# Mixture-of-experts stage: overflow branch behind the eighth pair, unread products, a gather with two writes per bank turn, and a reordered router

## The chip, the cores and the metric

The kernel runs on one core of a Trainium2 chip. A core has five engines with queues of their own: TensorE for matrix products (PE, its weight loads shown apart as PEld), VectorE (DVE), ScalarE (ACT), GpSimd (POOL) and SyncE (SP), which here issues nearly all DMAs. The metric is the device time of one execution in microseconds (us). The kernel before takes 2117.66 us, the median of three runs between 2117.41 and 2118.54.

## The reference, cut to what matters

The program computes two blocks over 256 rows of 1024 columns. The first is a hybrid layer (three attention-like branches, merged by gates) followed by a hierarchical mixture of experts; the second holds two feed-forward parts, a gated unit and a stick-breaking attention. The change touches the mixture of experts alone. A router picks for each row one of four groups and in it the two best of eight experts; all products are dense in the reference, with gates that are zero for the experts that were not picked.

```python
x = x + gt1 * (merged @ w_out)
h2 = rmsnorm(x, norm2_g) * (1.0 + sc2) + sh2
group_logits = h2 @ rg_w + rg_b
g_sel = argmax(group_logits)
exp_logits = (h2 @ re_w + re_b).reshape(-1, 4, 8)
in_group = exp_logits of group g_sel
top_v, top_i = lax.top_k(in_group, 2)
gates = softmax(top_v) * softmax(group_logits)[g_sel], at the picked experts
hg = silu(h2 @ w_gate[e]) * (h2 @ w_up[e])          # 1024 -> 512, 32 experts
y = sum over e of (hg * gates[:, e]) @ w_down[e]    # 512 -> 1024
x = x + gt2 * y
```

The weights of the experts are 32 x 3 matrices of 1024 x 512 (or 512 x 1024) numbers in f32, 201 MB of the 500 MB that the kernel reads.

## The kernel before

**Weights.** The expert weights come as 192 loads of 1 MB (tile 128 x 2048, half of a matrix), each issued by load_slot (L1200) on SP. There are 17 slots (names we, wx, ws, whl, wp by the memory they share); 17 loads go out ahead of the stage, the next one for a slot goes out when the products that read it are done. SP takes its queue in order, so a load that waits for its slot holds those behind it.

**Router.** route() runs once the residual rows x are final. TensorE transposes the two row tiles (turn, L1297), the results are copied out of PSUM to xT (evac: L1305 on ACT, L1303 on DVE; xT shares the buffer named whd), eight products per row tile give the 36 logits (L1313), and DVE scales them by the row's norm (rs, made on POOL in L1316) in L1317. Then a row of small DVE operations finds the experts (sel, L1363), TensorE counts each row's place in its expert's list (L1366 to L1370), and DVE makes the rank. The normed rows are kept as two parts of reduced precision, hh (tile hi, on ACT, L1331 and L1339) and hl (tile lo, on DVE, L1332 and L1364).

**Gather.** Each expert has a list of at most C rows. For four experts at a time, places() (L1158) builds a one-hot matrix from the rank, and gather() multiplies it with the rows: for each of eight column blocks k four products (L1172: hi and lo of two row tiles) into half of a PSUM bank, read by one ACT operation (L1174) into xg. Two blocks k share a bank. Four k make a half gather. The first half of the first gather stands before the first expert product; its second half stands in pair 0 after the first two loads are used; later halves stand one in each pair, a group of four experts ahead.

**Pairs.** Two experts form a pair, each on half of the array's columns. A pair has six calls of both() (L1211), each of which reads two loads in 16 products of 512 columns and then issues two loads: four for gate and up, then two for down. Between them stand the activation, the transposes (L1235, L1242), the half gather (ahead) and the previous pair's spread (L1264, eight products that put the results back to their rows). A list of the PE instructions (self.pe) is chained, so that the scheduler keeps their order.

**Overflow.** After pair p = 0 the kernel flushes that pair's spread, starts a new PE list, and calls overflow(): every engine loads the longest list's length (topi, L1407) and, if it is over C, goes through a slow loop for the rest (L1413). With these inputs it is not: the branch is only jumped over. By the built program SP holds at the end of the branch until every DMA that it issued has landed, which the rows in the next sections show.

**After the stage** residual() adds the result to x, and the first feed-forward part begins with transposes (L419).

Of the kernel before, what the change touches and what calls it, by code (L numbers as in the profile page):

```python
# [8 lines left out]
F32 = mybir.dt.float32  # L9
# [3 lines left out]
AF = mybir.ActivationFunctionType  # L13
OP = mybir.AluOpType
# [6 lines left out]
KT = D // 128  # L21
# [11 lines left out]
NB8 = 9  # L33
WS, WHL, WH2 = 3, 3, 3
NE_B8, NE_MIX, NSLOT = 7, 4, 17
ADA_EVERY, ADA_FROM = 3, 6
FRONT = 4
PADS = 320, 128, 128, 224
# [143 lines left out]
class Program:  # L182
# [280 lines left out]
    def run(self):  # L463
        tc, nc, d = self.tc, self.nc, self.d
        with ExitStack() as es:
            self.main = es.enter_context(tc.tile_pool(name="main", bufs=1))
            self.small = es.enter_context(tc.tile_pool(name="small", bufs=1))
            self.pad(self.small, PADS[0], "pad0")
            self.stg = es.enter_context(tc.tile_pool(name="stg", bufs=3))
            self.psum = es.enter_context(tc.tile_pool(name="psum", bufs=4, space=PSUM))  # L470
            self.dram = es.enter_context(tc.tile_pool(name="scr", bufs=1, space=DRAM))
            main = self.main
            self.cm = main.tile([128, KT], F32, name="cm")
            nc.sync.dma_start(self.cm, d["c"])
            self.x = main.tile([128, 2, 1024], F32, name="x")
            for t in range(2):
                nc.sync.dma_start(self.x[:, t], d["x"][t * 128:t * 128 + 128])
            k0 = main.tile([128, 256], F32, name="k0")
            nc.sync.dma_start(k0, d["k0"])
            self.ident, self.anti = k0[:, :128], k0[:, 128:]  # L480
            self.ones = main.tile([128, 128], F32, name="ones")
            nc.vector.memset(self.ones, 1.0)
            self.mhalf = main.tile([128, 32], F32, name="mhalf")
            nc.vector.memset(self.mhalf, -0.5)
            self.cc = main.tile([128, d["cols"].shape[1]], F32, name="cc")
            nc.sync.dma_start(self.cc, d["cols"])
            self.hi, self.lo = [main.tile([128, KT, S], F32R, name=n) for n in ("hi", "lo")]
            self.modscr = self.dram.tile([6, 1024], F32, name="modscr")
            self.rowp = es.enter_context(tc.tile_pool(name="rowp", bufs=1))
            self.km = self.rowp.tile([128, 320], F32, name="km")  # L490
            eights = ExitStack()
            self.exs = eights.enter_context(tc.tile_pool(name="exs", bufs=1))
            self.slots = [self.exs.tile([128, 2048], F32, name="wp")]
            self.units = [(2 * p + j, u) for p in range(NE // 2) for u in range(6) for j in range(2)]
            self.nload = self.nuse = 0
            self.pad(self.exs, PADS[1], "pad1")
            self.b8p = eights.enter_context(tc.tile_pool(name="b8", bufs=1))
            with tc.tile_pool(name="mix", bufs=1) as self.mix:
                self.hybrid()
            fg = self.row(self.rowp, d["rows"][0:1], name="fg", tag="row", bufs=2)  # L500
            self.experts()
            eights.close()
            self.whx = es.enter_context(tc.tile_pool(name="whx", bufs=1))
            self.pad(self.whx, PADS[2], "pad2")
            self.ffn(0, fg)
            self.dbg("f0", self.x)
            with tc.tile_pool(name="sgu", bufs=1) as self.sgup:
                self.sgu()
            self.dbg("m0", self.x)
            self.ffn(1)  # L510
            self.kvp = es.enter_context(tc.tile_pool(name="kv", bufs=1))
            with tc.tile_pool(name="kvt", bufs=1) as kvt:
                self.ffn(2, between=self.kv(kvt))
            self.dbg("f1", self.x)
            with tc.tile_pool(name="sb", bufs=1) as self.sbp:
                self.stick()
            self.dbg("m1", self.x)
            g = self.row(self.rowp, d["rows"][1:2], name="fing", tag="row", bufs=2)
            self.ffn(3)
            self.last_norm(g)  # L520
# [615 lines left out]
    def experts(self):  # L1136
# [5 lines left out]
        with tc.tile_pool(name="exw", bufs=1) as self.exw:  # L1142
# [20 lines left out]
            def gather(q, ks):  # L1163

                oh, xg = ohs[q], xgs[q % 2]
                parts = [(hz, t) for t in range(2) for hz in (self.hl, self.hh)]
                for k in ks:
                    if k % 2 == 0:
                        both = self.mms().rearrange("p (k a c) -> p k a c", k=2, a=4)
                    ps = both[:, k % 2]  # L1170
                    for i, (hz, t) in enumerate(parts):
                        self.chain(self.pe, nc.tensor.matmul(ps, hz[:, t, k * 128:k * 128 + 128], oh[:, t], start=(i == 0), stop=(i == 3)))  # L1172
                    gain, shift = self.a2c[:, k:k + 1], self.sh2c[:, k:k + 1]
                    nc.scalar.activation(xg[:, k], ps, AF.Identity, bias=shift, scale=gain)  # L1174

            places(0)
            gate, rgs = gates()
# [2 lines left out]
            for p in range(NE // 2):  # L1180
                q, ks = p // 2 + 1, range(4 * (p % 2), 4 * (p % 2) + 4)

                def ahead():
                    if 4 * q < NE:
                        if p % 2 == 0:
                            places(q)
                        gather(q, ks)

                pend = self.pair(p, xgs[p // 2 % 2], ohs[p // 2], gate, yp, pend, ahead, gather)
                if p == 0:  # L1190
                    self.spread(*pend)
                    pend, self.pe = None, []
                    self.overflow(topi, rgs, iota)
            self.spread(*pend)
            self.residual(yp, self.gt2)

    def load_slot(self):

# [68 lines left out]
    def route(self, km):  # L1267
# [27 lines left out]
        def turn(t, q):  # L1295
            for k in range(4 * q, 4 * q + 4):
                ins = nc.tensor.transpose(pss[t][q][:, (k % 4) * 128:(k % 4) * 128 + 128], self.x[:, t, k * 128:k * 128 + 128], self.ident)  # L1297
            return ins

        def evac(t, q):  # L1300
            c = xT[:, t, 4 * q:4 * q + 4].rearrange("p a b -> p (a b)")
            if q and t:
                self.chain(edge[0], V.tensor_copy(c, pss[t][q]))  # L1303
            else:
                self.chain(edge[1], nc.scalar.copy(c, pss[t][q]))  # L1305

        def square(t, h):
            self.chain(edge[1], nc.scalar.activation(junk, self.x[:, t, h * 512:h * 512 + 512], AF.Square, accum_out=ss[:, t, h:h + 1]))

        def logits(t):  # L1310
            pl = pss[t][0][:, :36]
            for k in range(KT):
                nc.tensor.matmul(pl, xT[:, t, k], self.rwa[:, k], start=(k == 0), stop=(k == KT - 1))  # L1313
            V.tensor_scalar(ss[:, t, 0:1], ss[:, t, 0:1], 1.0 / D, EPS, op0=OP.mult, op1=OP.add)
            V.scalar_tensor_tensor(ss[:, t, 1:2], ss[:, t, 1:2], 1.0 / D, ss[:, t, 0:1], op0=OP.mult, op1=OP.add)
            ins = nc.gpsimd.tensor_tensor(out=rs[:, t:t + 1], in0=ss[:, t, 1:2], in1=self.mhalf[:, :1], op=OP.pow)  # L1316
            V.scalar_tensor_tensor(lg[:, t], pl, rs[:, t:t + 1], self.base, op0=OP.mult, op1=OP.add)  # L1317
            return ins
# [8 lines left out]
        turn(1, 0)  # L1327
        square(1, 0)
        self.res(1, 1)
        logits(0)  # L1330
        self.chain(edge[1], nc.scalar.activation(hh[:, 0], self.x[:, 0], AF.Copy, scale=rs[:, 0:1]))  # L1331
        self.chain(edge[0], V.scalar_tensor_tensor(hl[:, 0], self.x[:, 0], rs[:, 0:1], hh[:, 0].bitcast(F32), op0=OP.mult, op1=OP.subtract))  # L1332
        evac(1, 0)
        turn(1, 1)
        evac(1, 1)
        square(1, 1)
        logits(1)
        self.chain(edge[1], nc.scalar.activation(junk[:, :1], self.ones[:, :1], AF.Exp))
        self.chain(edge[1], nc.scalar.activation(hh[:, 1], self.x[:, 1], AF.Copy, scale=rs[:, 1:2]))  # L1339
        self.res = self.rest = self.edge = None  # L1340
# [22 lines left out]
        found = V.tensor_mul(sel.rearrange("p a (g e) -> p a g e", g=4), og4, ssel[:, :, None, :].to_broadcast([128, 2, 4, 8]))  # L1363
        self.no_sync(V.scalar_tensor_tensor(hl[:, 1], self.x[:, 1], rs[:, 1:2], hh[:, 1].bitcast(F32), op0=OP.mult, op1=OP.subtract), found)  # L1364
        pk = self.mms()[:, :2 * NE].rearrange("p (a b) -> p a b", a=2)
        nc.tensor.matmul(pk, earlier, sel, start=True, stop=False)  # L1366
        nc.tensor.matmul(pk[:, 1], ones, sel[:, 0], start=False, stop=True)
        pt = self.mms()[:, :NE]
        for t in range(2):
            nc.tensor.matmul(pt, ones, sel[:, t], start=(t == 0), stop=(t == 1))  # L1370
        rank = small.tile([128, 2, NE], F32, name="rank")
        V.tensor_scalar(rank, sel.bitcast(F32), -1000.0, 1000.0, op0=OP.mult, op1=OP.add)
        V.tensor_add(rank, rank, pk)
# [463 lines left out]
```

## Time and profile before

| what | value |
|---|---|
| median of 3 runs | 2117.66 us |
| profiled execution | 2117.89 us |
| its span in the trace | 2116.1 us (1.8 us lie outside) |
| PE busy | 2033.4 us, 96% of the span |
| DVE, ACT busy | 53%, 40% |
| HBM read | 500.14 MB, 237 GB/s over the span |
| DMA in slices 16 to 21 of 40 (about 800 to 1100 us) | 421 GB/s, all engines busy |

The page cuts the span into 40 slices of 52.9 us. PE is busy in nearly all of them; in the slices of the expert stage, from about 700 to 1105 us, DMA is busy throughout as well, and nowhere else is it. The routed part before that, about 626 to 656 us, is a stretch of short operations that wait for one another. So two things are to be read apart there: which engine's work comes last in the expert stage, and when its loads start to flow.

### The profile page before, as it was taken

To read this page: it belongs to the slowest core of one execution; us is meant where nothing else is said; L and a number is where in the kernel's file an instruction comes from. 1 tells how busy PE (TensorE), PEld (TensorE's weight loads), DVE (VectorE), ACT (ScalarE), POOL (GpSimd) and SP (SyncE) were. 2 spreads that over 40 slices of the span, in tenths; PEclk is the share of its full clock that TensorE was granted. 3 is DMA by queue.
4 is the path that set the end of the run, shared out by engine and by line. 5 is a ranking of instruction groups with operands and counts; after the bars stand their busy time and mean duration, and the time that the engine had idled before them with its cause. 6 is when DMAs were issued, how large, how long until landed. Compare 5 with 4: busy or idle time off the path is not lost.

```text
span 2116.1 us, 29342 instructions
## 1 busy us (share of the span) xinstructions
PE 2033.4 (96%) x12228; PEld 1611.2 (76%) x12228; DVE 1111.7 (53%) x1596; ACT 846.8 (40%) x1200; POOL 25.0 (1%) x40
## 2 busy tenths in 40 slices
PE   7999999999997999999989999999999999999998
PEld 5889889778773344344438998879999999989997
DVE  5887876755551011101008556656555755685555
ACT  4454334344442111111116445545444644475443
POOL 0000000000000000000000000000000000000000
PEclk9999999999998999999999999999999999999999
DMA  8655545465485899999995555545555555534552
GB/s 328 237 192 205 182 157 220 169 238 201 169 346 234 362 421 421 421 421 421 421 412 191 185 194 199 212 158 177 182 190 189 177 183 181 179 120 144 196 182 97
DMA packets 72124, 503.17 MB, mean 238 GB/s; under 512 B 8218, under 2 KB 10034, under 8 KB 11698
## 3 DMA queue, kind: packets, MB, share of 16 engines
q1 hardware_dynamic: 71986, 501.24, 62.1%
q8 instruction: 98, 1.61, 0.3%
q14 instruction: 40, 0.33, 0.0%
HBM read 500.14 MB, written 1.07 MB: 237 GB/s over the span
## 4 chain that ended last, share of the span: by engine, by line
PE 58%; DMA 6%; ACT 1%; DVE 1%; issue 0%; POOLq 0%; DVEq 0%; POOL 0%; ACTq 0%; SPq 0%
PE mm L1211 11%; PE mm L276 10%; PE mm L278 10%; PE mm L277 10%; PE bg L276 5%; PE bg L277 5%; PE bg L278 5%; DMA wx<-in_w_e 3%; DMA we<-in_w_e 2%; PE bg L1264 1%; DMA wp<-in_w_e 1%; PE mm L1172 1%; ACT xg L1174 1%; PE mm L419 1%; PE mm L1789 0%
## 5 line engine op out<-in xcount | busy, mean ns | idle before, releaser
L256 DVE TENSOR_TENSOR whl<-ws,whl 128x1024 fp32r<-128x1024 f32 x228 | 277.7, 1220 | 225.0 <-ACT whl L255 224.2
L255 ACT CAST whl<-ws 128x1024 fp32r<-128x1024 f32 x228 | 238.3, 1048 | 300.5 <-PE mm L278 252.4
L256 DVE TENSOR_TENSOR wlx<-ws,whx 128x1024 fp32r<-128x1024 f32 x165 | 201.0, 1222 | 136.6 <-ACT whx L255 136.2
L255 ACT CAST whx<-ws 128x1024 fp32r<-128x1024 f32 x165 | 172.3, 1049 | 170.4 <-PE mm L278 96.0
L276 PE MATMUL mm<-hi,whl 128*128 128x256 f32 x836 | 235.4, 282 | 1.1 <-DVE whl L256 1.0
L277 PE MATMUL mm<-lo,whl 128*128 128x256 f32 x836 | 233.8, 280 | 0.1
L278 PE MATMUL mm<-hi,whl 128*128 128x256 f32 x836 | 233.3, 279 | 0.0
L256 DVE TENSOR_TENSOR whd<-ws,whd 128x1024 fp32r<-128x1024 f32 x113 | 137.7, 1219 | 113.7 <-ACT whd L255 112.8
L255 ACT CAST whd<-ws 128x1024 fp32r<-128x1024 f32 x113 | 118.2, 1046 | 174.4 <-PE mm L278 127.9
L276 PE MATMUL mm<-hi,wlx 128*128 128x256 f32 x640 | 178.7, 279 | 0.5 <-ACT rrow L1554 0.5
L277 PE MATMUL mm<-lo,whx 128*128 128x256 f32 x640 | 178.5, 279 | 0.0
L278 PE MATMUL mm<-hi,whx 128*128 128x256 f32 x640 | 178.5, 279 | 0.0
L276 PEld LDWEIGHTS mm<-hi,whl 128*128 128x128 f32 x836 | 157.2, 188 | 3.2 <-issue 1.2
L277 PEld LDWEIGHTS mm<-lo,whl 128*128 128x128 f32 x836 | 157.2, 188 | 1.5 <-DVE lo L616 0.7
L278 PEld LDWEIGHTS mm<-hi,whl 128*128 128x128 f32 x836 | 157.1, 188 | 0.1
L1230 DVE TENSOR_TENSOR act<-act,mm 128x512 f32<-128x512 f32 x16 | 11.0, 688 | 230.9 <-PE mm L1211 230.9
L276 PEld LDWEIGHTS mm<-hi,wlx 128*128 128x128 f32 x640 | 120.3, 188 | 1.9 <-ACT rrow L1554 0.8
L277 PEld LDWEIGHTS mm<-lo,whx 128*128 128x128 f32 x640 | 120.3, 188 | 0.8
L278 PEld LDWEIGHTS mm<-hi,whx 128*128 128x128 f32 x640 | 120.3, 188 | 0.0
L277 PE MATMUL mm<-whl,hi 128*128 128x512 f32 (+1 forms) x304 | 118.0, 388 | 0.0
L278 PE MATMUL mm<-whl,hi 128*128 128x512 f32 (+1 forms) x304 | 116.3, 383 | 0.0
L276 PE MATMUL mm<-whl,lo 128*128 128x512 f32 (+1 forms) x304 | 115.2, 392 | 1.1 <-DVE lo L433 1.1
(552 smaller groups left out, 4240.5 us busy)
## 6 DMA issues: line engine op xcount, KB each, us to landing
ws<-in_w_fi SPq DMA_DIRECT2D x88, 1024.0 KB, 4.8
we<-in_w_e SPq DMA_DIRECT2D x81, 1024.0 KB, 19.8
wx<-in_w_e SPq DMA_DIRECT2D x44, 1024.0 KB, 19.8
ws<-in_w_fo SPq DMA_DIRECT2D x44, 1024.0 KB, 4.8
ws<-in_w_a SPq DMA_DIRECT2D x40, 1024.0 KB, 4.8
ws<-in_w_e SPq DMA_DIRECT2D x33, 1024.0 KB, 19.5
ws<-in_w_b SPq DMA_DIRECT2D x26, 1024.0 KB, 4.8
whl<-in_w_e SPq DMA_DIRECT2D x22, 1024.0 KB, 19.8
```

Of the source, the lines that this page charges most:

```text
L255: w1 = nc.scalar.copy(wh[:, :m], src)
L256: w2 = nc.vector.tensor_sub(wl[:, :m], src, wh[:, :m].bitcast(F32))
L276: first = mm(out, ll, rh, start=start, stop=False)
L277: mm(out, lh, rl, start=False, stop=False)
L278: self.last_mm = mm(out, lh, rh, start=False, stop=stop)
L419: ins = nc.tensor.transpose(pss[k % 2][:, (k // 2) * 128:(k // 2) * 128 + 128], self.x[:, t, k * 128:k * 128 + 128], self.ident)
L1172: self.chain(self.pe, nc.tensor.matmul(ps, hz[:, t, k * 128:k * 128 + 128], oh[:, t], start=(i == 0), stop=(i == 3)))
L1174: nc.scalar.activation(xg[:, k], ps, AF.Identity, bias=shift, scale=gain)
L1211: self.chain(self.pe, self.nc.tensor.matmul(ps[j * 64:j * 64 + 64], xs[:, k, j], ws[j][:, o:o + 512], start=(k == 0), stop=(k == last)))
L1230: V.tensor_mul(a, a, ps[1])
L1264: self.chain(self.pe, self.nc.tensor.matmul(yp[t][h], ot[:, t * 128:t * 128 + 128], part[:, h], start=(p == 0 and i == 0), stop=(p == NE / ...
```

## The change

Five edits, all in route() and experts():

- The branch (with the flush of the spread and the new PE list) moves from behind pair 0 to behind pair 7 (P_OVER = 7).
- gather() does the eight products of two blocks k, then the two ACT reads. Before, the read of the first block stood between its four products and those of the second, in the same bank.
- warm(n) issues n products of ident with the constant k0 (128 x 256 in f32) into a PSUM tile that nobody reads: 7 behind the second row tile's logits, 4 behind the counting products, 3 behind the last spread.
- logits(0) is split: products 0 to 3, then the transposes turn(1, 1), then products 4 to 7.
- evac(1, 0) goes ahead of hh of row tile 0 on ACT, evac(1, 1) ahead of hl of row tile 0 on DVE; the PE instructions of the router join the chained list.

```diff
+P_OVER = 7
@@ gather()
-                for k in ks:
-                    if k % 2 == 0:
-                        both = self.mms().rearrange("p (k a c) -> p k a c", k=2, a=4)
-                    ps = both[:, k % 2]
-                    for i, (hz, t) in enumerate(parts):
-                        self.chain(self.pe, nc.tensor.matmul(ps, hz[:, t, k * 128:k * 128 + 128], oh[:, t], start=(i == 0), stop=(i == 3)))
-                    gain, shift = self.a2c[:, k:k + 1], self.sh2c[:, k:k + 1]
-                    nc.scalar.activation(xg[:, k], ps, AF.Identity, bias=shift, scale=gain)
+                for k2 in ks[::2]:
+                    ps = self.mms().rearrange("p (k a c) -> p k a c", k=2, a=4)
+                    for k in (k2, k2 + 1):
+                        for i, (hz, t) in enumerate(parts):
+                            self.chain(self.pe, nc.tensor.matmul(ps[:, k - k2], hz[:, t, k * 128:k * 128 + 128], oh[:, t], start=(i == 0), stop=(i == 3)))
+                    for k in (k2, k2 + 1):
+                        gain, shift = self.a2c[:, k:k + 1], self.sh2c[:, k:k + 1]
+                        nc.scalar.activation(xg[:, k], ps[:, k - k2], AF.Identity, bias=shift, scale=gain)
@@ experts()
-                if p == 0:
+                if p == P_OVER:
                     self.spread(*pend)
                     pend, self.pe = None, []
                     self.overflow(topi, rgs, iota)
             self.spread(*pend)
+            self.warm(3, self.pe, "mm")
             self.residual(yp, self.gt2)
+
+    def warm(self, n, order=None, tag="bg"):
+        ps = self.mms(tag=tag)
+        for _ in range(n):
+            ins = self.nc.tensor.matmul(ps[:, :256], self.ident, self.k0, start=True, stop=True)
+            if order is not None:
+                self.chain(order, ins)
+        return ins
@@ route()
-        logits(0)
-        self.chain(edge[1], nc.scalar.activation(hh[:, 0], self.x[:, 0], AF.Copy, scale=rs[:, 0:1]))
-        self.chain(edge[0], V.scalar_tensor_tensor(hl[:, 0], self.x[:, 0], rs[:, 0:1], hh[:, 0].bitcast(F32), op0=OP.mult, op1=OP.subtract))
+        logits(0, range(4))
         evac(1, 0)
         turn(1, 1)
+        logits(0, range(4, KT))
+        self.chain(edge[1], nc.scalar.activation(hh[:, 0], self.x[:, 0], AF.Copy, scale=rs[:, 0:1]))
         evac(1, 1)
+        self.chain(edge[0], V.scalar_tensor_tensor(hl[:, 0], self.x[:, 0], rs[:, 0:1], hh[:, 0].bitcast(F32), op0=OP.mult, op1=OP.subtract))
         square(1, 1)
         logits(1)
+        self.warm(7, self.pe)
...
+        self.warm(4, self.pe)
```

On PE, in the router, the queue of the kernel before reads as follows, from the transposes of the second row tile (L1297) over the logits (rwa is the routers' weight, whd is xT) and the counting products to the first gather product:

```order
L1297 MATMUL mm<-k_75,x 128x128 x4
L1313 MATMUL mm<-rwa,whd 128x36 x8
L1297 MATMUL mm<-k_75,x 128x128 x4
L1313 MATMUL mm<-rwa,whd 128x36 x8
L1366 MATMUL mm<-sel,before_r 128x64
L1367 MATMUL mm<-sel,ones_r 128x32
L1370 MATMUL mm<-sel,ones_r 128x32 x2
```

and the queue of the changed kernel, whose lines lie 11 to 16 further down:

```order
L1308 MATMUL mm<-k_75,x 128x128 x4
L1325 MATMUL mm<-rwa,whd 128x36 x4
L1308 MATMUL mm<-k_75,x 128x128 x4
L1325 MATMUL mm<-rwa,whd 128x36 x12
L1203 MATMUL bg<-k_75 128x256 x7
L1382 MATMUL mm<-sel,before_r 128x64
L1383 MATMUL mm<-sel,ones_r 128x32
L1386 MATMUL mm<-sel,ones_r 128x32 x2
L1203 MATMUL bg<-k_75 128x256 x4
```

The last transposes have moved up by four products, and eleven unread products stand between the logits, the counting and the gather.

On DVE, in the router, from the last residual sum to the second row tile's logits (lo is hl, whd is xT), the queue before is

```order
L1570 TENSOR_TENSOR x<-x,tmp 128x512
L1314 TENSOR_SCALAR ssr<-ssr 128x1
L1317 SCALAR_TENSOR_TENSOR lg<-mm,rsr,rbase 128x36
L1332 SCALAR_TENSOR_TENSOR lo<-x,rsr,hi 128x1024
L1303 COPY whd<-mm 128x512
L1315 SCALAR_TENSOR_TENSOR ssr<-ssr 128x1
L1317 SCALAR_TENSOR_TENSOR lg<-mm,rsr,rbase 128x36
```

and that of the changed kernel

```order
L1587 TENSOR_TENSOR x<-x,tmp 128x512
L1328 TENSOR_SCALAR ssr<-ssr 128x1
L1315 COPY whd<-mm 128x512
L1331 SCALAR_TENSOR_TENSOR lg<-mm,rsr,rbase 128x36
L1350 SCALAR_TENSOR_TENSOR lo<-x,rsr,hi 128x1024
L1329 SCALAR_TENSOR_TENSOR ssr<-ssr 128x1
L1331 SCALAR_TENSOR_TENSOR lg<-mm,rsr,rbase 128x36
```

The copy that the second row tile's logits need has moved ahead of the long subtraction.

On SP, around the branch, the loads of the kernel before are these (the compare is the start of the overflow branch, and twelve loads of pair 0 stand ahead of it):

```order
L1200 DMA wp<-in_w_e 128x2048
L1200 DMA we<-in_w_e 128x2048 x7
L1200 DMA wx<-in_w_e 128x2048 x4
L1413 COMPARE_AND_BRANCH
L1414 DMA rgscr<-rgs 128x32x4
```

and of the changed kernel these:

```order
L1211 DMA wx<-in_w_e 128x2048 x4
L1211 DMA ws<-in_w_e 128x2048 x3
L1211 DMA whl<-in_w_e 128x2048 x2
L1211 DMA wp<-in_w_e 128x2048
L1211 DMA we<-in_w_e 128x2048 x7
L1211 DMA wx<-in_w_e 128x2048 x3
L1430 COMPARE_AND_BRANCH
L1431 DMA rgscr<-rgs 128x32x4
```

The compare now stands behind the twelve loads of pair 7, the 113th load of the 192, where before it stood behind the 29th.

## Rows read from the trace of the kernel before

**Rows 1.** Chain of waits, longest pieces: start us, us, what.
```profile
710.22 20.75 PE mm L1211 x96
...
737.98 20.75 PE mm L1211 x96
...
977.41 19.82 DMA wx<-in_w_e
```

**Rows 2.** Stage windows: us; PE, PEld, DVE, ACT, POOL busy; PEclk; DMA; GB/s.
```profile
652.00:659.00 7.00, 5.69 (x32) 3.00 (x30) 0.00 (x0) 2.16 (x4) 0.00 (x0) 1.00 0.76 286
659.00:663.00 4.00, 4.00 (x20) 1.29 (x18) 0.00 (x0) 1.88 (x2) 0.00 (x0) 1.00 0.40 133
677.00:680.00 3.00, 3.00 (x16) 0.86 (x12) 0.75 (x1) 0.52 (x1) 0.00 (x0) 1.00 0.73 238
680.00:689.00 9.00, 2.75 (x12) 1.61 (x12) 0.75 (x1) 0.69 (x1) 0.00 (x0) 0.77 0.94 391
689.00:695.00 6.00, 6.00 (x23) 1.94 (x23) 0.00 (x0) 0.00 (x0) 0.00 (x0) 0.77 0.05 15
695.00:700.00 5.00, 5.00 (x26) 1.85 (x24) 0.00 (x0) 0.60 (x1) 0.00 (x0) 1.00 0.92 370
700.00:1105.00 405.00, 378.01 (x1842) 164.41 (x1840) 40.19 (x79) 68.78 (x124) 0.00 (x0) 1.00 1.01 421
```

**Rows 3.** Expert loads, 700 to 1090: count, KB, median us to landing.
```profile
we<-in_w_e SPq DMA_DIRECT2D x67, 1024.0 KB, 19.8
```

**Rows 4.** DVE and POOL timelines, router: start us, us, operation, [idle <-releaser].
```profile
636.00 0.26 DVE L1317 SCALAR_TENSOR_TENSOR lg<-mm,rsr,rbase 128x36 f32<-128x36 f32 x1 [2.02 <-PE mm L1313]
...
634.06 0.55 POOL L1316 TENSOR_TENSOR rsr<-ssr,mhalf 128x1 f32<-128x1 f32 x1 [5.02 <-DVE ssr L1315]
```

**Rows 5.** PE timeline, router and first pair.
```profile
639.29 0.39 PE L1366 MATMUL mm<-sel,before_r 128*128 128x64 f32 x1 [3.41 <-DVE sel L1363]
...
641.71 0.55 PE L1172 MATMUL mm<-oh,lo 128*128 128x256 f32 x1 [1.41 <-DVE oh L1158]
...
647.44 1.12 PE L1211 MATMUL mm<-wp,xg 128*64 128x512 f32 x1
...
652.68 0.39 PE L1172 MATMUL mm<-oh,lo 128*128 128x256 f32 x1
...
653.02 0.28 PE L1172 MATMUL mm<-oh,lo 128*128 128x256 f32 x1
653.14 0.28 PE L1172 MATMUL mm<-oh,hi 128*128 128x256 f32 x1
...
656.61 7.95 PE L1211 MATMUL mm<-we,xg 128*64 128x512 f32 x36
```

**Rows 6.** Windows of the router, columns as in Rows 2.
```profile
634.00:635.00 1.00, 1.00 (x5) 1.00 (x6) 0.00 (x0) 0.83 (x3) 0.55 (x1) 0.50 0.29 119
650.00:651.00 1.00, 1.00 (x6) 0.37 (x4) 0.00 (x0) 0.00 (x0) 0.00 (x0) 0.60 0.00 0
```

**Rows 7.** One line: an f32 product of 256 columns.
```profile
L1694 PE MATMUL mm<-kvx,k x4: 377/378/379, 1749.0 to 1749.7; 128*128 128x256 f32 x4
```

**Rows 8.** Line L1413, the branch: ns min/median/max, first and last start us.
```profile
L1413 SPq EVENT_SEMAPHORE  x8: 17/17/17, 686.1 to 690.7; - x8
...
L1413 SPq COMPARE_BRANCH  x1: 50/50/50, 681.1 to 681.1; - x1
...
L1413 PEldq COMPARE_BRANCH  x1: 5952/5952/5952, 682.4 to 682.4; - x1
```

**Rows 9.** SP and PE timelines behind the branch.
```profile
693.90 3.76 SPq L1200 DMA_DIRECT2D ws<-in_w_e  x3
...
688.77 5.53 PE L1211 MATMUL mm<-ws,xg 128*64 128x512 f32 x17 [5.77 <-PEq L1413]
```

**Rows 10.** PE timeline and a window at the next part.
```profile
1115.03 1.09 PE L419 MATMUL mm<-k,x 128*128 128x128 f32 x4 [1.63 <-DVE x L1570]
...
1118.00:1122.00 4.00, 3.98 (x19) 3.99 (x20) 3.25 (x9) 2.62 (x7) 0.00 (x0) 0.52 0.30 113
```

More of the change, by code (lines that the diff above doesn't have):

```diff
@@ L479, in run @@
             nc.sync.dma_start(k0, d["k0"])
-            self.ident, self.anti = k0[:, :128], k0[:, 128:]
+            self.k0, self.ident, self.anti = k0, k0[:, :128], k0[:, 128:]
             self.ones = main.tile([128, 128], F32, name="ones")
@@ L1297, in turn @@
                 ins = nc.tensor.transpose(pss[t][q][:, (k % 4) * 128:(k % 4) * 128 + 128], self.x[:, t, k * 128:k * 128 + 128], self.ident)
+            self.chain(self.pe, ins)
             return ins
@@ L1308, in square, with logits @@
             self.chain(edge[1], nc.scalar.activation(junk, self.x[:, t, h * 512:h * 512 + 512], AF.Square, accum_out=ss[:, t, h:h + 1]))
-        def logits(t):
+        def logits(t, ks=range(KT)):
             pl = pss[t][0][:, :36]
-            for k in range(KT):
-                nc.tensor.matmul(pl, xT[:, t, k], self.rwa[:, k], start=(k == 0), stop=(k == KT - 1))
+            for k in ks:
+                self.chain(self.pe, nc.tensor.matmul(pl, xT[:, t, k], self.rwa[:, k], start=(k == 0), stop=(k == KT - 1)))
+            if ks[-1] < KT - 1:
+                return
             V.tensor_scalar(ss[:, t, 0:1], ss[:, t, 0:1], 1.0 / D, EPS, op0=OP.mult, op1=OP.add)
@@ L1365, in route @@
         pk = self.mms()[:, :2 * NE].rearrange("p (a b) -> p a b", a=2)
-        nc.tensor.matmul(pk, earlier, sel, start=True, stop=False)
-        nc.tensor.matmul(pk[:, 1], ones, sel[:, 0], start=False, stop=True)
+        self.chain(self.pe, nc.tensor.matmul(pk, earlier, sel, start=True, stop=False))
+        self.chain(self.pe, nc.tensor.matmul(pk[:, 1], ones, sel[:, 0], start=False, stop=True))
         pt = self.mms()[:, :NE]
         for t in range(2):
-            nc.tensor.matmul(pt, ones, sel[:, t], start=(t == 0), stop=(t == 1))
+            self.chain(self.pe, nc.tensor.matmul(pt, ones, sel[:, t], start=(t == 0), stop=(t == 1)))
+        self.warm(4, self.pe)
         rank = small.tile([128, 2, NE], F32, name="rank")
```

## The prediction, made before the kernel ran

> **What bounds the kernel now.** I read the chain of waits first, because only it says whose work ends last. Through the expert stage its long pieces are the pairs' products, one every 27.76 us (710.22 to 737.98), until 977.41; from there the pieces are loads of expert weights, each 19.82 us from issue to landing [rows 1]. The reader is to see that the sequence changes hands. The windows say why: from 700 to 1105 the DMA share is 1.01 at 421 GB/s [rows 2]. A load of 1.0486 MB takes 2.49 us at that rate, and since one lands in 19.8 us [rows 3], eight are in flight. Twelve loads, a pair's, take 29.9 us, TensorE needs 27.76: it lives off the 17 loads fetched ahead, uses them up, and at 977 waits. So the stage ends when the last load has come, however the chain draws its early part. That load comes at a fixed time after the stream has started, plus every gap in it. Two numbers then set the time: when the first slots are released, and how long DMA stands idle afterwards.
>
> Idle DMA, worked out as width x (1 - GB/s / 421) [rows 2]: 652 to 659 2.2 us, of which 1.75 are the first load's own way; 659 to 663 2.74; 677 to 680 1.30; 680 to 689 0.64; 689 to 695 5.79; 695 to 700 0.61. Without the 1.75 this is 11.6 us.
>
> **The change part by part.** *Router order.* The second logits' scaling starts at 636.00, when TensorE's last logits product is done; the factor it also needs leaves POOL at 634.06 + 0.55 = 634.61 [rows 4]. With the transposes and the copy moved forward the products end before that, so POOL is what is late next: 634.75 instead of 636.00, -1.25 us. ACT's and DVE's long operations of row tile 0 are now behind the copies, which could delay the norm (that chain goes ACT, DVE, POOL) by a copy of about 0.6 to 1; bounds -1.4 to +0.3.
>
> *Gather.* The first half gather goes from 641.71 to the first expert product at 647.44, 5.73 us, at half clock; the second from 652.68 to 656.61, 3.93 us, at full clock [rows 5]. At full clock a product follows the one before by 0.12 (653.02, 653.14), so 16 take 1.9 us and with a first one's 0.2 a half is 2.1. The rest was TensorE waiting for ACT to leave the bank. What is late next: ACT reads four blocks in about 0.56 each, but into two banks, so TensorE only waits for the last two reads before the first expert product needs them, and products k = 0 come first. I take 2.1; if ACT's last read is waited for, 2.9.
>
> *Clock.* The granted clock was half from 634 on (0.50 in 634 to 635, while TensorE was busy all of that microsecond) and came back within 650 to 651 (0.60) [rows 6], after the expert products had run without a pause from 647.44 [rows 5]. The first call of both(), 16 products, took 5.24 us there (647.44 to 652.68); at full clock 16 of 96 in 20.75 us [rows 1] are 3.46. Eleven unread products now fill the stretch. One is two passes; four passes start 0.23 apart (1749.0 to 1749.7, four in all) [rows 7], so 0.47 for a product: seven take 3.3, four 1.9, three 1.4 us at full clock, twice that at half. The seven run from about 634.2; the counting product, now at 639.29 - 1.25 = 638.0, finds them gone if the clock is full (637.5), and waits to 639.2 if half of them go at half clock (1.65 us more). I take the middle, +0.6, with 0 and +1.2 as ends. If the clock stays low over all seven (6.5 us) it is +2.7, and +4.7 if the four (3.7 us) reach past the gather's start as well. The four lie beside DVE's rank and one-hot, 639.5 to 640.5.
>
> The Trainium skill (TensorE: Matmul & The Clock Gate, Part 1: The HAM clock gate) says that the clock's resting state is the throttled one and that activity releases it. By that rule the seven products meet half clock themselves and cost their double price before anything is gained. The rows agree as far as they go: the expert products from 647.44 ran at half for their first microseconds. It is the +1.2 end above, and the sum by it alone would be 0.6 us higher.
>
> With the clock back by then, the first half gather takes 2.1 for 5.73, -3.6, and the first both() 3.46 for 5.24, -1.8. If the clock is still low, a half gather takes twice 1.9, 3.8: -1.9, and both() gains 0. So the first slots are released 1.25 - 0.6 + 3.6 + 1.8 = 6.05, say 6.0 us earlier; bounds 8 earlier and 3 later (+0.3 + 4.7 - 1.9). Everything of the stream moves with them.
>
> *Second release.* The idle 2.74 of 659 to 663 is there since two loads last 5 us and the next slots come free only behind the second half gather (3.93) and another both(). With 2.1 for 3.93 the gap is 0.9: -1.8. The 1.30 of 677 to 680 stands behind pair 0's own half gather in the same way: 0.3, -1.0.
>
> *Branch.* What it does to DMA: SP compares at 681.1, waits for the eight semaphores until 690.7 [rows 8], and issues again at 693.90, when TensorE, late itself, has released a slot [rows 9]. The three rows 680 to 700 lose 0.64 + 5.79 + 0.61 = 7.0. Behind pair 7 SP drains eight loads instead of the few of before, but draining is work, not idleness. TensorE, by then waiting for loads, has slots free, so the 3.2 us from 690.7 to 693.90 fall to one issue, 0.3: 4.1 lost, -2.9. Bounds: 0 lost if SP fetches code and issues so that the queue never runs dry, and 9.1 if SP's own 5.0 us from compare to first semaphore (681.1 to 686.1) come behind the drain and not beside it.
>
> What it does to TensorE: held 5.95 us at the jump, then at half clock (5.53 us for 17 products from 688.77) [rows 8, 9]. Behind pair 7 that and the flush lie in time in which TensorE waits for loads. Its cover: a pair loses 2.0 of its 27.76 with the gather, 25.8 against 29.9, so eight pairs that remain give 32 us back.
>
> *Also hidden* are the fourteen other half gathers, about 2 us each: on TensorE's side of the stage, not on DMA's. Were TensorE the bound, they would bring 28.
>
> *Next part.* Three products behind the last spread, 1.4 us, lie in the 1.63 that TensorE waits for DVE's x before 1115.03; the clock is half there (0.52 in 1118 to 1122) [rows 10]. If it rises 1.4 us sooner, half of that is gained: -0.7, bounds 0 and -1.8.
>
> *Sum*: -6.0 (start) - 1.8 - 1.0 - 2.9 (gaps) - 0.7 = -12.4. Against the profiled execution, 2117.89 (span 2116.1, 1.8 outside): 2105.5; that lies 0.2 above the median 2117.66, so 2105.2.
>
> **The rivals.** *Clock still low at the gather* (chance 0.17): the unread products come in two short groups with a pause for sel between, and a low clock outlasted a busy microsecond at 634; for the forecast speaks that continuous products brought it back. With all seven at half, the start is -1.25 + 2.7 - 1.9 = -0.45 instead of -6.0: 2110.8.
>
> *SP's code fetch behind the drain* (0.13): for it, SP's 5.0 us followed the compare at once, when loads were still outstanding, so it lay beside the drain; against the forecast, a longer drain with more queued could put the fetch last. +5.0: 2110.2.
>
> *The queue never runs dry* (0.12): if SP's wait ends load by load and issues overlap, 4.1 go: 2101.1. Against it, the order of the instructions holds all eight waits ahead of the next load.
>
> *Only the small edits act* (0.05): the clock low, the products late by 4.7, the router's factor by 0.3: start +3.1, branch at its worst (9.1 for 7.0, +2.1), second release -1.8, pair 0's gap -1.0, next part 0: +2.4, 2120.1, within 0.2% of before.
>
> *TensorE held long at the jump* (0.03), which would make it slower: its 5.95 us fell while DMA ran at 391 GB/s with a queue that was emptying. Behind eight queued loads the code could wait for them too, 19.8 + 5.95 = 26 us. That is still less than the 32 of cover; it decides from a hold over 32 + 12.4 = 44, at 50 the time is 2123. Against it: nothing in the rows shows a fetch even near that.
>
> The Trainium skill (DMA: Bandwidth & Descriptors, Queues, rings and completion order) says that a DMA engine goes round its queue rows packet by packet. By that rule a code fetch in a row of its own doesn't wait for all queued loads, and the hold stays of the size seen. No run here shows it yet.
>
> **How the numbers follow.** Forecast 0.50, 2105.2; low clock 0.17, 2110.8; late fetch 0.13, 2110.2; no dry queue 0.12, 2101.1; small edits 0.05, 2120.1; held 0.03, 2123. The likeliest's own range is 2102 to 2108. The range 2098.5 to 2112 takes in the start's better end (-8, and -1.8 in the next part) with a full queue, and both slower rivals on this side; late fetch and low clock together, 2115.8, stay out. A measurement tells 0.2%, 4.2 us, from no change: faster 0.92, same 0.05, slower 0.03.
>
> **What would show it.** Second logits on DVE about 1.2 us earlier; the granted clock full at the first gather product; the first half gather in 2.1 us, no wait for ACT inside; the first both() done some 6 us before 652.68; one dip of DMA at about 860 to 890, 4 us wide, none at 690; each pair 25.8 us until TensorE runs into its loads, well before 977; the last load about 12 us earlier. The forecast is wrong if DMA has a second dip, if TensorE instead of a load ends the stage, or if the clock is half at 641.

## The result: 14.6 us faster, and the profile after

Six runs of the changed kernel gave a median of 2103.51 us (2100.70 to 2105.84), six of the kernel before beside them 2118.10 (2115.33 to 2121.01). The ratio is 0.9931 with a 95% interval of 0.9918 to 0.9944: 14.6 us less, between 11.9 and 17.4. The forecast was 12.4 less, 2105.2.

The two profiled executions are 15.65 us apart (2117.89 and 2102.24; spans 2116.1 and 2100.5). Loads are counted from 0: number 16 is the last of those fetched ahead, number 17 the first that waits for a slot, 191 the last. Their issue times cut the span into pieces:

| piece | before | after | difference | forecast |
|---|---|---|---|---|
| start to issue of load 16 (nothing changed there) | 628.45 | 626.68 | -1.8 | 0 |
| **A** load 16 to load 17: router, gather, first both() | 24.32 | 17.94 | -6.4 | -6.0 |
| **B** load 17 to load 191: the stream with its gaps | 433.98 | 426.64 | -7.3 | -5.7 |
| **C** load 191 to the end of the span | 1029.34 | 1029.24 | -0.1 | -0.7 |

The first row is chance: the code up to there is the same, and over all the runs below load 16 went out between 624.9 and 627.5.

The chain of waits of the changed kernel (start us, us, what) against [rows 1]:

```profile
862.78 3.65 PE mm L1222 x7
...
868.17 15.67 PE mm L1222 x57
...
891.85 10.35 DMA ws<-in_w_e
902.26 19.86 DMA we<-in_w_e
...
1061.32 19.82 DMA wp<-in_w_e
...
1087.99 7.11 PE mm L1222 x32
```

Loads, not TensorE, make up the chain from 891.85 on, where before that began at 977.41. TensorE now runs into its loads early: a pair takes 25.8 us as forecast (its transposes, L1246, start at 683.89 and 709.66), but from 813.9 to 843.8, and again from 937.6 on, 29.8, the time of twelve loads. The two pairs right behind the branch take 25.8 and 27.1 and win back what TensorE stood there. What it saved inside the pairs is not in the time.

The router, from the DVE, POOL and PE timelines of the changed kernel (start us, us, operation, [idle <-releaser]), against [rows 4, 5]:

```profile
632.67 0.26 DVE L1331 SCALAR_TENSOR_TENSOR lg<-mm,rsr,rbase 128x36 f32<-128x36 f32 x1 [0.67 <-POOL rsr L1330]
```

```profile
632.08 0.56 POOL L1330 TENSOR_TENSOR rsr<-ssr,mhalf 128x1 f32<-128x1 f32 x1 [4.81 <-DVE ssr L1329]
```

```profile
632.11 4.83 PE L1203 MATMUL bg<-k 128*128 128x256 f32 x14
636.60 0.38 PE L1382 MATMUL mm<-sel,before_r 128*128 128x64 f32 x1
...
638.77 0.47 PE L1172 MATMUL mm<-oh,lo 128*128 128x256 f32 x1
...
640.94 0.64 PE L1222 MATMUL mm<-wp,xg 128*64 128x512 f32 x1
...
644.53 0.39 PE L1172 MATMUL mm<-oh,lo 128*128 128x256 f32 x1
...
646.62 10.52 PE L1222 MATMUL mm<-we,xg 128*64 128x512 f32 x48
```

Take the 1.8 us of a head start off each. The second logits are scaled at 632.67, 1.6 us earlier, and what they wait for is POOL's factor. The counting starts at 636.60, just as the unread products end (632.11 + 4.83 modelled, the next starts behind the last): 0.9 earlier, so the products hold it up by 0.6. The first gather takes 638.77 to 640.94, 2.17 us for 5.73, with no wait for ACT inside; the first both() ends at 644.53, 3.59 for 5.24.

Windows of the same kernel (PE, PEld, DVE, ACT, POOL busy; PEclk; DMA share; GB/s) against [rows 6] and [rows 2]:

```profile
633.00:634.00 1.00, 1.00 (x4) 0.73 (x4) 0.87 (x7) 0.92 (x2) 0.00 (x0) 0.50 0.01 4
636.00:637.00 1.00, 1.00 (x8) 0.90 (x6) 1.00 (x2) 0.00 (x0) 0.00 (x0) 1.00 0.03 8
644.00:651.00 7.00, 7.00 (x42) 3.48 (x40) 0.00 (x0) 2.58 (x5) 0.00 (x0) 1.00 0.76 290
651.00:655.00 4.00, 4.00 (x22) 1.40 (x20) 0.00 (x0) 1.27 (x2) 0.00 (x0) 1.00 0.93 342
655.00:668.00 13.00, 12.11 (x68) 5.80 (x66) 1.75 (x4) 3.61 (x7) 0.00 (x0) 1.00 1.00 413
668.00:671.00 3.00, 3.00 (x16) 1.01 (x14) 0.75 (x1) 0.69 (x1) 0.00 (x0) 1.00 1.01 404
692.00:860.00 168.00, 161.56 (x798) 70.07 (x794) 18.07 (x35) 30.05 (x55) 0.00 (x0) 1.00 1.01 421
886.00:889.00 3.00, 3.00 (x22) 2.16 (x23) 0.24 (x2) 2.34 (x5) 0.00 (x0) 1.00 0.37 153
889.00:892.00 3.00, 3.00 (x16) 1.00 (x14) 0.00 (x0) 0.40 (x1) 0.00 (x0) 1.00 0.21 36
892.00:895.00 3.00, 3.00 (x16) 1.01 (x14) 0.75 (x1) 0.29 (x1) 0.00 (x0) 1.00 0.82 311
```

The granted clock is half (0.50, which is 1.2 GHz) at 633, where the products run, and full (1.00, 2.4 GHz) at 636, before the gather. Of DMA's gaps the one before the second release is 0.75 us (4 x (1 - 342/421)) for 2.74, the one at pair 0's own gather 0.12 for 1.30, and the branch has made a single dip of 1.91 + 2.74 + 0.78 = 5.4 us for 7.0. Between these the rows are at 404 to 421 GB/s.

The branch itself (line L1430 is the old L1413; ns min/median/max, first and last start us), against [rows 8]:

```profile
L1430 SPq EVENT_SEMAPHORE  x8: 17/17/17, 887.9 to 890.8; - x8
...
L1430 PEldq COMPARE_BRANCH  x1: 6132/6132/6132, 856.2 to 856.2; - x1
...
L1430 SPq COMPARE_BRANCH  x1: 50/50/50, 870.9 to 870.9; - x1
```

TensorE is held 6.13 us at the jump, with eight loads queued, for 5.95 with few. SP waits from 870.9 to 887.9 for the first semaphore; the seventeen microseconds are the drain, and whatever fetching of code there was lies within. The first semaphore comes when load 111 lands (887.87), the other seven when load 112, the last, has landed (890.34), and load 113 goes out at 890.93.

### The profile page after: what moved, and what is told of

Read it like the earlier page. It is cut to its first block, busy times and chain, and to the rows that moved or that the text cites. A ratio compares the mean times of both kernels' runs of the same rounds, so it can differ in the third digit from the quotient of the medians.

```text
span 2100.5 us, 29412 instructions
## 1 busy us (share of the span) xinstructions
PE 2033.9 (97%) x12256; PEld 1609.3 (77%) x12256; DVE 1111.4 (53%) x1596; ACT 844.7 (40%) x1200; POOL 24.9 (1%) x40
## 4 chain that ended last, share of the span: by engine, by line
PE 47%; DMA 9%; DVE 2%; issue 1%; ACT 0%; POOLq 0%; DVEq 0%; POOL 0%; SPq 0%; ACTq 0%
PE mm L277 10%; PE mm L278 10%; PE mm L279 10%; PE bg L277 5%; PE bg L278 5%; PE bg L279 5%; DMA we<-in_w_e 4%; DMA wx<-in_w_e 3%; PE mm L1222 2%; DMA ws<-in_w_e 1%; DMA wp<-in_w_e 1%; PE mm L420 1%; DVE sn L1777 0%; PE mm L1806 0%; PE mm L450 0%
## 6 DMA issues: line engine op xcount, KB each, us to landing
we<-in_w_e SPq DMA_DIRECT2D x81, 1024.0 KB, 19.8
wx<-in_w_e SPq DMA_DIRECT2D x44, 1024.0 KB, 19.8
ws<-in_w_e SPq DMA_DIRECT2D x33, 1024.0 KB, 19.8
whl<-in_w_e SPq DMA_DIRECT2D x22, 1024.0 KB, 19.8
```

## Experiments

Each time is the median of 5 to 12 executions, the ratio is to the kernel before run beside them. An interval reaches 0.0009 to 0.0015 to each side, 2 to 3 us, so what is smaller is read from the trace of one execution, in the pieces A, B and C. Kernels with the same stage code differ in B by up to 2 us (427.7, 426.6, 426.5, 425.6), and kernels with the same code up to the first slot differ in A by up to 0.8 (17.43 to 18.24): that much is chance in one execution.

| run | median us | ratio to before, interval | A | B | C |
|---|---|---|---|---|---|
| changed kernel | 2103.51 | 0.9931 (0.9918 to 0.9944) | 17.94 | 426.64 | 1029.24 |
| branch_only | 2111.31 | 0.9973 (0.9963 to 0.9983) | 24.47 | 428.69 | 1029.32 |
| branch_back | 2103.98 | 0.9940 (0.9928 to 0.9953) | 17.45 | 428.55 | 1029.04 |
| branch_p14 | 2103.91 | 0.9933 (0.9920 to 0.9946) | 17.93 | 423.80 | 1033.09 |
| products_only | 2113.49 | 0.9981 (0.9972 to 0.9990) | 20.88 | 434.45 | 1030.44 |
| no_products | 2104.73 | 0.9936 (0.9922 to 0.9950) | 19.52 | 427.70 | 1029.27 |
| no_tail | 2102.94 | 0.9929 (0.9915 to 0.9943) | 17.93 | 425.55 | 1031.40 |
| old_gather | 2107.52 | 0.9949 (0.9935 to 0.9963) | 19.29 | 431.57 | 1029.02 |
| old_router | 2107.61 | 0.9952 (0.9938 to 0.9965) | 20.53 | 426.52 | 1030.80 |
| act_loads | 2102.82 | 0.9931 (0.9918 to 0.9944) | 17.45 | 426.00 | 1029.12 |
| pool_loads | 2103.25 | 0.9932 (0.9920 to 0.9944) | 17.43 | 427.77 | 1029.69 |
| pool_all | 2106.08 | 0.9948 (0.9934 to 0.9962) | 17.73 | 425.74 | 1032.44 |
| pool_mid | 2127.40 | 1.0050 (1.0035 to 1.0064) | 18.24 | 438.56 | 1041.81 |

**The branch alone** (the kernel before with one line changed):

```diff
-                if p == 0:
+                if p == 7:
```

> The kernel before with one edit: the overflow branch behind pair 7. If the stage ends with its last load (theory), only DMA's idle time at the branch counts: 7.0 us at 680 to 700 go, a dip of 4.4 us (as in the changed kernel, where the issue of load 113 fell 4.4 us behind) comes behind pair 7, all else as before: -2.6, 0.9988 of before. If TensorE's own stop is what cost (rival: 5.95 us held, some 3 us of flush, half clock afterwards), moving it under TensorE's waiting gives 9 us or more: 0.996 or less. If the place of the branch is indifferent: 1.000.

5.7 us less, between 3.6 and 7.8: between the two figures, nearer to neither. The trace decides. C is as before, so a load still ends the stage, and the gain is in B, 5.3. The dip behind pair 7, in windows of this run:

```profile
895.00:900.00 5.00, 3.99 (x26) 2.08 (x22) 1.00 (x3) 0.85 (x2) 0.00 (x0) 1.00 0.26 108
900.00:905.00 5.00, 3.71 (x22) 2.24 (x24) 0.00 (x0) 2.17 (x5) 0.00 (x0) 1.00 0.91 351
```

is 3.7 + 0.8 = 4.5 us, for 7.0 before: 2.5 by idle DMA. The other 2.8 of B are not idle DMA. What SP's queue (q1) moved from the issue of load 17 to the landing of load 191 shows where they are (packets, MB, share of the 16 engines): in the kernel before, then in this run, then in the changed kernel,

```profile
q1 hardware_dynamic: 25424, 185.20, 98.4%
...
q1 hardware_dynamic: 25274, 184.12, 99.0%
...
q1 hardware_dynamic: 25272, 184.10, 99.5%
```

where the 175 loads are 183.5 MB. What is over belongs to loads of the next part, which alone were issued behind load 191 in that time: before, 1.08 MB more of them, 2.6 us at 421 GB/s, went ahead of the end of load 191. Part of it arose in one step in the trace of before, where load 146 went out 4.01 us after load 145 (970.92, 974.93) for the usual 2.49, with neither TensorE nor SP late. Why the order slips is open; products_only, with the branch in its old place, has 185.06 MB, branch_back 184.45. So the idle time that the theory counts is worth 2.5 us, as it said, and another 2.6 are DMA time that went to other loads.

**The branch put back**:

```diff
-P_OVER = 7
+P_OVER = 0
```

> The changed kernel with the branch back behind pair 0. Theory: the dip behind pair 7 (4.4 us) goes, one of about 7 us at the branch comes back, since SP there waits for a TensorE that was held: +2.6 to the changed kernel, 2106, 0.9943 of before. Rival (TensorE's stop counts): +9, 2112.5, 0.9974.

B is 1.9 longer, the ratio 0.0009 (1.9 us) higher, within the intervals, so 0 and 2.6 us can't be told apart. TensorE's stop at the jump is here in the open and costs no 9 us, which speaks against the rival. With the other edits in place, then, the move of the branch is not shown to be worth anything in time.

**The branch behind pair 14** (P_OVER = 14):

> The changed kernel with the branch behind pair 14, when the last load has been issued. If only SP's drain counted, the 4.4 us go and nothing comes: 2099, 0.991 of before. Theory: TensorE's cover is gone there, since only one pair is left in which it can win back 4 us; held 6.1 us, flush 2.8, and products at half clock behind it (13.65 us of half clock were seen behind pair 7, so 3 to 7 us lost) make 12 to 16, less 4 of cover and 4.4 of drain: +3 to +8, 2107 to 2112, with TensorE and not a load at the stage's end.

Both things happened, and came out even: B is 2.8 shorter, since nothing is left to issue while SP drains, and C 3.9 longer. The chain of this run now ends in TensorE:

```profile
1071.97 16.08 PE mm L1222 x64
```

The size was put too high. TensorE stood 6.0 us at the jump and lost 2.1 at half clock (its first 16 products from there took 5.6 us for 3.5), 8 in all and not 12 to 16; C grew by 3.9 alone, and the rest, it seems, TensorE would have spent waiting for the last pair's loads, which it now found landed.

**The unread products** alone in the kernel before (there the router's PE instructions are chained as well, in their old order), and taken out of the changed one:

```diff
 products_only: kernel before
+        self.warm(7, self.pe)      # behind logits(1)
+        self.warm(4, self.pe)      # behind the counting products
 no_products: changed kernel
-        self.warm(7, self.pe)
-        self.warm(4, self.pe)
```

> The kernel before with the seven and four unread products alone (old router order, old gather, branch behind pair 0). The prediction's price for the clock: first half gather 3.93 for 5.73 us, first call of both() 3.5 for 5.24, less the counting held up by 1 us (the seven ended 639.95 in the run with the old order): about -2.6 in the trace up to the first load, 2115.1, 0.9988 of before. Rival (what the run without the products suggests, where a gather without pauses brought the clock back by itself and the products were worth 1.6): also here the clock comes back by itself within the gather, 0 to -1.

> The changed kernel without the seven and the four unread products in the router (the three behind the last spread stay). Theory: the granted clock stays at half over the counting and the first gather, as it did in the kernel before: first half gather 3.8 for 2.17 us, first call of both() 5.2 for 3.6, less some 0.6 by which the products held up the counting: +2.7 to the changed kernel, 2106, 0.9943 of before. Rival (the clock comes back without them, they only cost their time): -0.6, 2103.

In the kernel before they give 3.4 us in A (24.32 to 20.88) and 4.0 in time (2.1 to 5.9): the first theory. In the changed kernel they are worth 1.6 in A (19.52 to 17.94), between the two. PE timeline of the run without them:

```profile
637.97 0.58 PE L1172 MATMUL mm<-oh,lo 128*128 128x256 f32 x1 [1.32 <-DVE oh L1159]
638.35 0.42 PE L1172 MATMUL mm<-oh,hi 128*128 128x256 f32 x1
638.57 0.41 PE L1172 MATMUL mm<-oh,lo 128*128 128x256 f32 x1
...
641.69 1.10 PE L1222 MATMUL mm<-wp,xg 128*64 128x512 f32 x1
...
642.60 0.62 PE L1222 MATMUL mm<-wp,xg 128*64 128x512 f32 x1
...
643.05 0.59 PE L1222 MATMUL mm<-wp,xg 128*64 128x512 f32 x1
```

The gather without pauses starts at half clock (0.21 from product to product) and takes 3.72, but the clock is full again from the second step of both() (0.45 for 0.91). In the kernel before, with the old gather and its two pauses, it stayed low until 650 [rows 6]; the router's order differs between the two as well. So products and gather, it seems, in part do the same work; that their gains do not add is measured (3.4 and 1.6).

**The old gather in the changed kernel** (the lines of the diff undone):

> The changed kernel with the old gather (read of a block between the products of two that share its bank). Theory (loads end the stage): first half gather 3.93 for 2.17 us, +1.8; second half behind the first call of both(), +1.8 in the gap before the second release; pair 0's half, up to +1.0; the thirteen others hidden: +4.6 to the changed kernel, 2108, 0.9953 of before. Rival (TensorE ends the stage): 16 halves at 1.8 to 2: +30, 2133.

3.8 us by the two ratios (0.9949 and 0.9931), and the trace has 1.35 in A and 4.9 in B. The second is more than the 2.8 counted for the gaps, because the clock fell as well: within pair 0's half gather the products step at 0.21, as this PE timeline row and the next show,

```profile
663.50 0.41 PE L1173 MATMUL mm<-oh,lo 128*128 128x256 f32 x1
663.71 0.41 PE L1173 MATMUL mm<-oh,hi 128*128 128x256 f32 x1
...
666.79 8.48 PE L1222 MATMUL mm<-wx,actT 128*64 128x512 f32 x32
```

and two calls of both() from 666.79 take 8.3 us where two at full clock take 7. TensorE's 30 us are nowhere.

**The old router order in the changed kernel**:

> The changed kernel with the old order in the router (eight logits products together, copies of row tile 1 behind the long operations of row tile 0). Theory: second logits scaled 1.6 us later relative to the residual rows, everything behind follows, and the seven products start later too: +1.5, 2105, 0.9938 of before. Rival: TensorE's seven products, which then start later, hold the counting up more: +2.5.

A is 2.6 longer: the rival. The seven products start at 634.69 for 632.11, and the counting starts behind them at 639.95 for 636.60; the second logits alone are 1.55 later.

**The products behind the last spread** taken out:

> The changed kernel without the three unread products behind the last spread. What the prediction said: the clock at the next part returns 1.4 us or more later, +0.7. What the trace of the changed kernel suggests (the clock came back earlier, yet the products after 1410 stood 15.5 us earlier, no more than the last load): 0, within 0.3 in the trace, 2103.5.

Medians 0.6 us apart in favour of leaving them out, which is nothing at this interval. C is 2.2 longer, but 1.7 of that arose at 1854 to 1858, where the clock fell in this execution and not in the other; up to 1437 the difference behind the last load is 0.55. The products are worth between 0 and 0.6; the 0.7 is not shown.

**Can the dip be filled?** Four runs in which other engines issue some of the loads, in load_slot (the conditions written out in numbers):

```diff
-            ins = self.nc.sync.dma_start(...)
+            eng = self.nc.scalar if 113 <= self.nload < 117 else self.nc.sync       # act_loads
+            eng = self.nc.gpsimd if 113 <= self.nload < 117 else self.nc.sync       # pool_loads
+            eng = self.nc.gpsimd if self.nload >= 17 else self.nc.sync              # pool_all
+            eng = self.nc.gpsimd if 17 <= self.nload < 176 else self.nc.sync        # pool_mid
+            ins = eng.dma_start(...)
```

> The changed kernel, with the four loads that follow the branch (113 to 116) issued by ACT and not by SP. ACT passes the branch at 855 and has to wait for no load of SP's there, so it can issue while SP drains. Theory: DMA has no dip at 886 to 895, every later load comes 4.4 us earlier, -4.4: 2099, 0.991 of before. Rival: what stops DMA there is not SP's drain but slots that TensorE releases late (it was held 6 us), or ACT's activations are held up by loads that wait: the dip stays, 2103.5 or more.

No change. ACT was held: its timeline shows the issue at 888.10 and the next activation after 38 us without work,

```profile
888.10 0.38 ACTq L1212 DMA_DIRECT2D wx<-in_w_e  x1
...
890.04 0.60 ACT L1241 ACTIVATE act<-mm 128x512 f32<-128x512 f32 x1 [38.05 <-issue]
```

while SP passed its eight semaphores at the end of the branch between 885.3 and 888.2. In the trace ACT's loads wait for semaphores of these same eight: its first passes 0.04 us behind SP's update of one that it needs (887.98, 888.02), and not behind SP's last, as the next expectation has it. So ACT is tied to SP's drain because the two share these semaphores. It is no rule for every issuer, as POOL shows next.

> The changed kernel, with loads 113 to 116 issued by POOL, which passes the branch at 640 and has nothing else to do. With ACT as issuer the first of them went out at 888.10, 0.1 us after SP's last wait at the branch, so ACT was held by the semaphores that SP settles there, and the dip stayed. Theory: a queue of its own with semaphores of its own is free of that, the loads go out as TensorE frees their slots (867 to 880), the dip goes, -4.4: 2099, 0.991 of before. Rival: POOL's loads too wait for semaphores that SP settles behind the drain: they go out at 888, TensorE is not held by it as it was with ACT, 2103.5.

POOL's loads carry semaphores of their own and went out at 867.94 to 871.89, as hoped; so, counted from load 17, four slots were free 17 us before SP issued again in the changed kernel, in spite of TensorE's stop. But the dip only moved. Windows of this run:

```profile
888.00:892.00 4.00, 4.00 (x21) 1.54 (x18) 0.75 (x1) 0.69 (x1) 0.00 (x0) 1.00 1.01 420
892.00:896.00 4.00, 1.67 (x6) 0.19 (x2) 0.00 (x0) 0.00 (x0) 0.00 (x0) 1.00 0.73 299
896.00:900.00 4.00, 2.99 (x8) 0.93 (x10) 0.00 (x0) 0.00 (x0) 0.00 (x0) 0.68 0.08 33
900.00:904.00 4.00, 4.00 (x20) 1.34 (x18) 0.00 (x0) 0.60 (x1) 0.00 (x0) 0.89 0.69 242
```

1.2 + 3.7 + 1.7 = 6.6 us. One of SP's eight, issued at 865.67, landed at 896.97, 31.3 us later for the usual 19.8, so SP's drain ended 10 us later. Two queues share the bandwidth. The Trainium skill says so too (DMA: Bandwidth & Descriptors, Issuing engines are not separate DMA queues): transfers end up on the same engines and interleave, whoever issued them. The trace agrees, with those 31.3 us.

> The changed kernel, with all 175 loads behind the first 17 issued by POOL. With four loads on POOL the dip only moved: SP's own eight loads shared the bandwidth with POOL's and ended 10 us later, and the queue was dry again behind them. Theory: with no load of SP's own under way SP's drain holds nothing, POOL passes the branch at 640, so loads flow from pair 0 to pair 15 without a dip: 4 to 5 us less, 2098.5, 0.9908 of before. Rival: POOL needs longer than SP for a load (0.55 to 1.1 us were seen against 0.33) or its eight semaphores release later, so that the stream is below 421 GB/s: 1% less would already take the 4 us back, 2103 or more.

Here the dip is gone, as the theory said; windows of this run over the branch:

```profile
880.00:890.00 10.00, 9.15 (x55) 4.87 (x53) 1.00 (x3) 3.57 (x7) 2.23 (x5) 1.00 1.02 423
890.00:900.00 10.00, 10.00 (x50) 3.36 (x48) 1.50 (x2) 1.13 (x3) 2.17 (x5) 1.00 1.01 418
```

and POOL's 0.54 us for an issue cost nothing. Load 182 landed 419.9 us after the issue of load 17, for 424.1 in the changed kernel: the gain is there. (B doesn't show it: POOL issued a load 17.1 us ahead of its landing, SP 19.8.) But the time is not below the changed kernel's (ratio 0.9948 for 0.9931), and C is 3.2 longer. SP, with no expert loads to issue, sent loads of the next part at 1069.95, as its timeline row shows, and they took their share while TensorE waited for the last expert loads (PE timeline):

```profile
1069.95 27.64 SPq L220 DMA_DIRECT2D ws<-in_w_fi  x4
```

```profile
1080.16 1.12 PE L1223 MATMUL mm<-wp,xg 128*64 128x512 f32 x1 [3.90 <-DMA wp<-in_w_e]
```

The last load landed at 1094.39, 24.5 us after its issue; in the changed kernel at 1091.08.

> As the run with all 175 later loads on POOL, but loads 176 to 191 go back to SP. In that run the dip at the branch was gone (419 to 423 GB/s from 860 to 900), and the last loads landed 5 us apart for 2.5, since SP, which had nothing else to issue, had already sent three loads of the next part that took their share. Theory: with the last sixteen loads ahead of these in SP's queue, the order is as before at the end and the gain at the branch stays: 4.4 us less than the changed kernel, 2099, 0.9910 of before. Rival: POOL's and SP's loads under way side by side delay the early ones, TensorE stops for them and the end is no earlier: 2103 or more.

The rival, and more than it said. POOL's last loads, needed first, landed 4.97 us apart (1054.27, 1059.24, 1064.20, 1069.17) for 2.49, since SP's sixteen, needed later, ran beside them. DMA was busy to the end, with the wrong loads; windows of this run:

```profile
1060.00:1080.00 20.00, 12.21 (x36) 3.20 (x34) 0.00 (x0) 0.60 (x1) 0.00 (x0) 0.84 1.01 420
1080.00:1100.00 20.00, 19.89 (x90) 8.02 (x88) 2.50 (x5) 2.33 (x4) 0.00 (x0) 0.93 0.26 101
```

From 1080 TensorE has many landed loads to work off, while DMA has little to do. The span ends 25 us later, and the gain at the branch is lost several times over. No version was found that beats the changed kernel beyond its interval.

## Why the prediction was right, and where it was off

- **What bounds the stage**: right, shown from three sides. Old gather in 16 half gathers costs 4 to 6 us and not 30; TensorE's stop of 6 us at the jump costs nothing behind pair 7, where POOL found slots free 17 us before SP's next issue, and no more than 1.9 in B behind pair 0, where SP's restart is in it; a stage whose last loads come later ends later (pool_all), whatever TensorE has saved.
- **Start, -6.0**: measured -6.4 in the trace. Router -1.25 forecast, 1.6 measured, products late 0.6 as forecast, gather 2.17 us for 2.1, first both() 3.59 for 3.46. The seven did meet half clock, from 631.9 to 635.3 by the trace. The bound of 8 us has no working: the best ends of its terms give 1.4 + 3.6 + 1.8 = 6.8. What the sum did not say is that its terms overlap: products alone give 3.4, while removing them from the changed kernel costs 1.6, the old order 2.6, the old gather 1.35.
- **Gaps before and at pair 0, -2.8**: 2.0 and 1.2 by the windows, 3.2.
- **Branch, -2.9**: 7.0 for 5.4 by idle DMA, so 1.6; the step that was mis-sized is the dip of 4.1. It took the loss inside the drain from one with few loads, 680 to 690, and held that "draining is work, not idleness"; with eight in flight the rate falls to 153 GB/s from 886 on, while the last load lands only at 890.34. By time the move alone is worth 3.6 to 7.8; with the other edits in place it is 1.9, not clear of chance (branch_back).
- **What no term had**: B is shorter by 7.3, of which 4.8 are idle DMA and 2.6 are the 1.1 MB of the next part's loads that no longer went ahead of load 191 (185.20 and 184.10 MB). Their cause stays open. That 12.4 came near 13.8 is therefore in part luck: 1.3 too much at the branch and 0.6 at the next part stand against these 2.6 and 0.8 too little at the start and at the two gaps.
- **Next part, -0.7**: failed. The clock did return sooner (half from 1102.9 to 1106.3, for 1115.0 to 1121.9), and counted from load 191 TensorE stood 0.6 us earlier when it was back (1102.94 for 1119.03). But by 1141 only 0.15 of that was left, and the end of the span did not follow: -0.1. What took it up is open.
- **The rivals**: clock still low at the gather: no, 1.00 at 636. SP's fetch behind the drain: no, SP's semaphores come with the landings of loads 111 and 112, and 0.6 us behind the second load 113 is on its way. The queue that never runs dry: no, 36 GB/s in 889 to 892. TensorE held long: no, 6.13 us; in it two packets of kind instruction were moved in queues of their own (q14 at 858.27, q8 at 859.86), beside the loads. The Trainium skill's rule on queue rows (DMA: Bandwidth & Descriptors, Queues, rings and completion order), by which a code fetch doesn't wait for all queued loads, agrees with that. That the whole 6 us are a code fetch no run shows.

## What to carry to other kernels

Find which queue's last item ends a stage; a wait removed from the other engine is then worth only what it brings forward the first release or closes in that queue. A branch whose body is jumped over can still cost: here SP waited 17 us for all its transfers, and a second issuer for the gap was no free way out, because its transfers shared the bandwidth and overtook those that were needed first. Edits that raise the same clock must be priced together, since the second one finds the work done.

## What was not expected

- An expert load sometimes falls 1.2 to 1.5 us behind for good in the middle of a full stream, with all later loads shifted (before at load 146, branch_p14 at load 133). DMA does not pause there: from 970.85 to 982.32 before, four loads landed (4.19 MB) and 4.80 MB were moved, so loads behind them ran ahead. It is not tied to any instruction here; its cause is open. It moves a single execution by as much as some of the edits.
- Unread products at half clock, 4.6 to 5.6 us for seven, were still a gain, since the clock was back before the gather.
- Two queues side by side kept DMA at 420 GB/s to 1080 and yet cost 24 us against the changed kernel: what was needed first came late.
